# Where the copies, the sums of squares and the end of a rope stand in an attention layer on one core

## The chip, the cores and the metric

The kernel runs on one core of a Trainium2 chip. The metric is the device time of one execution in microseconds (us); less is better. The core has TensorE (PE in the profile, with its weight loads as PEld), VectorE (DVE), ScalarE (ACT), GpSimd (POOL) and SyncE (SP, used here only to issue DMAs). Each engine works through its own queue in order, and DMAs are issued as entries of such a queue.

## What is computed

An encoder trunk of two layers over 16 learned meta tokens and 512 tokens of width 2048 (T = 528): layer 0 is grouped-query softmax attention with 16 query heads, 8 key and value heads of width 128, normalised q and k and rotary positions; layer 1 is gated linear attention. The change is in layer 0 only, in how q and k are made:

```python
def _rotate(x, ang):
    cos, sin = jnp.cos(ang), jnp.sin(ang)          # per token
    x1, x2 = jnp.split(x, 2, axis=-1)
    return jnp.concatenate([x1 * cos - x2 * sin, x2 * cos + x1 * sin], axis=-1)
...
    q, k, v, gate = jnp.split(h @ w_in, [...], axis=-1)
    q = apply_axial_rope(rmsnorm(q, q_norm), ang_row, ang_col)
    k = apply_axial_rope(rmsnorm(k, k_norm), ang_row, ang_col)
    p = softmax(q @ k.T * ATTN_HEAD_DIM ** -0.5)
    return ((p @ v) * silu(gate)) @ w_out
```

`apply_axial_rope` rotates the first 64 of the 128 dimensions by the token's row and the last 64 by its column, so the partner of a dimension is the one 32 further or 32 back. `rmsnorm` divides by the root of the mean square over the 128 dimensions of a head.

## The kernel before

Every factor of a product is kept as a pair of tiles, high and low part (`uh`, `ul`; `split` writes the high part on ACT and the low part on DVE), and a product takes three matmuls. Activations lie transposed, 128 dimensions on the partitions and the 528 tokens along the row, in two halves of 264 (`HALVES`). `project` makes one block of 128 columns of `h @ w_in`: for each half a bank of PSUM (the chip has eight; `ps_p` is a ring of three of them, tag "pp"), 16 x 3 matmuls (L152 to L154), and then `evac`. Weights come in units of 8 k-blocks through `weights` (load L147 on SP's queue, split L129 on ACT and L130 on DVE), high and low parts in rings of three.

Attention goes over eight groups g, each with one key head and two query heads. While the softmax and the products of group g run (`attention`), `qkv(g + 1)` projects k, the first q and the second q of the next group, and then its v. Each of the three goes through `take` and `rope`: `evac` copies the block to `qw` and its squares to `sq` (L286, L287, on ACT); four DMAs (L294) copy `qw` with its blocks of 32 partitions swapped to `qs`; `sq` is split into `sh`, `sl`; POOL multiplies `qw` by the cosine (L299) and `qs` by the sine (L300). Two functions come later: `sums`, once per half, where PE adds the squares over the partitions (L304, L305, with a matrix of ones) and DVE reads the bank into `f` (L307); and `late`, which takes the inverse root on ACT (L133, L134), adds the two rotated parts (L311) and multiplies by the root (L312) on DVE, and splits the result into the tiles that attention reads (`kh`, `kl`, `qh`, `ql`). There are 24 ropes: three of the first group, whose blocks were projected at the kernel's start (`first_group`), and three in each `qkv`.

Attention of a group has 9 blocks of queries: the score product (L613 to L615, in the one pair of banks of `ps_s`, "s"), the maximum (L618), the exponential (L621), the scaling (L623, L624), the transposes (L631, L633, in a ring of two banks, `ps_t`, "t", which v's transposes use too), their split (L635, L636), and the product with v (L651 to L654) in `ps_o`, "o", which is a single bank. The sums of squares use that bank as well. Two gates per group are loaded from DRAM (L587), multiplied by the row's norm (L591), go through a SiLU (L137 to L139 on ACT, L601 on POOL), multiply the group's output (L595) and are stored (L596, on POOL's queue).

What is emitted when is set by `Clock`: `clk.step` moves a clock by the modelled time of each projection matmul, and `clk.after(dt, fn)` puts a function into the program once the clock has moved on by dt. The numbers in `rope`'s calls and the first value that `lead` yields (how long attention of a group waits for its start) are such times. The clock counts projection matmuls only, so a unit of it is longer than a microsecond wherever attention lies between. Behind that a scheduler sets the final order on each engine, and `tc.high_priority` lets an instruction go ahead of others.

Of the kernel before, what the change touches and what calls it, by code (L numbers as in the profile page):

```python
# [10 lines left out]
F32 = mybir.dt.float32  # L11
# [8 lines left out]
P = 128  # L20
# [7 lines left out]
HALVES = ((0, HALF), (HALF, T))  # L28
# [54 lines left out]
def hybrid_encoder(  # L83
# [5 lines left out]
    nc = tc.nc  # L89
    V, A, G, PE = nc.vector, nc.scalar, nc.gpsimd, nc.tensor  # L90
    clk = Clock()

    def pool(stack, name, bufs=1, **kw):
        return stack.enter_context(tc.tile_pool(name=name, bufs=bufs, reuse_waits="tile", **kw))
# [5 lines left out]
    ps_p = pool(ctx, "ps_p", 3, space=PSUM)  # L100
# [18 lines left out]
    def col(i):  # L119
        return cols[:, i:i + 1]  # L120
# [7 lines left out]
    def split(hi, lo, src):  # L128
        A.copy(hi, src)  # L129
        V.tensor_tensor(lo, src, hi.bitcast(F32), op=ALU.subtract)  # L130

    def rsqrt_inplace(t):
        A.activation(t, t, AF.Ln)  # L133
        A.activation(t, t, AF.Exp, scale=-0.5)  # L134
# [21 lines left out]
    def project(src, c0, parts, evac, last_k=None, ws=None):  # L156

        ws = ws or [weights(src[:, k0:k0 + 8, c0:c0 + P]) for k0 in (0, 8)]
        for a, b in parts:
            ps = ps_p.tile([P, 512], F32, tag="pp", name="pp")[:, :b - a]  # L160
            for k in range(KT):
                wh, wl = ws[k // 8]
                three(ps, wh[:, k % 8], wl[:, k % 8], k, a, b, k == 0, k == KT - 1)
                clk.step(3 * (b - a + 7) / 2400)
                if last_k and (a, b) == parts[-1]:
                    last_k(k)
            evac(ps, a, b)
# [111 lines left out]
    def take(wcol):  # L279

        qws.append(qws.pop(0))
        qw = qws[-1]
        sq = wk.tile([P, T], F32, tag="sq", name="sq")

        def evac(ps, a, b):
            A.activation(qw[:, a:b], ps, AF.Copy, scale=wcol)  # L286
            A.activation(sq[:, a:b], ps, AF.Square)  # L287
        return qw, sq, evac

    def rope(qw, sq, outs, steps):  # L290
        qs = wk.tile([P, T], F32, tag="qs", name="qs")
        for b in range(4):
            s = b ^ 1
            nc.scalar.dma_start(out=qs[b * 32:b * 32 + 32, :], in_=qw[s * 32:s * 32 + 32, :])  # L294
        sh = wk.tile([P, T], F32R, tag="sh", name="sh", bufs=1)
        sl = wk.tile([P, T], F32R, tag="sl", name="sl", bufs=1)
        split(sh, sl, sq)
        f = sq
        G.tensor_tensor(qw, qw, cos, op=ALU.mult)  # L299
        G.tensor_tensor(qs, qs, sin, op=ALU.mult)  # L300

        def sums(a, b):
            ps = ps_o.tile([P, 512], F32, tag="o", name="ssq")[:, :b - a]
            PE.matmul(ps, ones_r, sh[:, a:b], start=True, stop=False)  # L304
            PE.matmul(ps, ones_r, sl[:, a:b], start=False, stop=True)  # L305
            with tc.high_priority(AHEAD):
                V.scalar_tensor_tensor(f[:, a:b], ps, 1.0 / P, erow[:, a:b], op0=ALU.mult, op1=ALU.add)  # L307

        def late():
            rsqrt_inplace(f)  # L310
            V.tensor_tensor(qw, qw, qs, op=ALU.add)  # L311
            V.tensor_tensor(qw, qw, f, op=ALU.mult)  # L312
            for hi, lo, a, b in outs:
                split(hi, lo, qw[:, a:b])
        for step, part in zip(steps, HALVES):
            clk.after(step, lambda part=part: sums(*part))
        clk.after(8.3, late)

    def qk_tiles(p, n):
        kh, kl = [p.tile([P, T], F32R, name=f"k{w}{n}") for w in "hl"]  # L320

        qh, ql = [p.tile([P, 2 * T], F32R, name=f"q{w}{n}") for w in "hl"]
        outs = ([(kh, kl, 0, T)], [(qh[:, :T], ql[:, :T], 0, T)],
                [(qh[:, Q1:], ql[:, Q1:], 0, SEQ), (qh[:, T:Q1], ql[:, T:Q1], SEQ, T)])
        return (qh, ql, kh, kl), outs
    Q1 = T + META

    qws = [c0.tile([P, T], F32, name=f"qw{i}") for i in range(3)]
# [6 lines left out]
    ps_t = pool(st, "ps_t", 2, space=PSUM)  # L335
# [43 lines left out]
    accs, banks = [], []  # L379
    for i, (si, off) in enumerate(((0, 0), (1, 0), (1, P))):  # L380
        for j, (a, b) in enumerate(HALVES):
            n = 2 * i + j
            if n < 3:
                ps = ps_p.tile([P, 512], F32, tag="pp", name="pp")
            else:
                ps = ps_g.tile([P, 512], F32, name=f"g{n}")
            ps = ps[:, :b - a]
# [27 lines left out]
    ssq = sp.tile([P, 5, 4], F32, name="ssq")  # L415
# [103 lines left out]
    qks = [qk_tiles(pk, i) for i in range(2)]  # L519
# [3 lines left out]
    ps_t = pool(ps0, "ps_t0", 2, space=PSUM)  # L523
    ps_o = pool(ps0, "ps_o", space=PSUM)
# [15 lines left out]
    def values(g):  # L540
        vh = wa.tile([P, 4, P], F32R, tag="vh", name="vh")
        vl = wa.tile([P, 4, P], F32R, tag="vl", name="vl")
        vm = vm_bufs[g % 2]
        if g:
            project(w_in0, 3072 + g * P, HALVES, lambda ps, a, b: A.copy(vt[:, a:b], ps))

        def late():
            ps = ps_t.tile([P, 512], F32, tag="t", name="vps")
            for t in range(4):
                PE.transpose(ps[:, t * P:(t + 1) * P], vt[:, t * P:(t + 1) * P], ident)  # L550
            for t in range(4):
                pst = ps[:, t * P:(t + 1) * P]
                A.activation(vh[:, t, :], pst, AF.Copy, scale=rcol[:, t:t + 1])
                V.scalar_tensor_tensor(vl[:, t, :], pst, rcol[:, t:t + 1], vh[:, t, :].bitcast(F32),
                                       op0=ALU.mult, op1=ALU.subtract)
            pm = ps_t.tile([P, 512], F32, tag="t", name="vpm")[:META, :P]
            PE.transpose(pm, vt[:, SEQ:T], ident)
            rm = rcol[:META, 4:5]
            A.activation(vm[0:META], pm, AF.Copy, scale=rm)
            A.activation(vm[64:64 + META], pm, AF.Copy, scale=rm)  # L560
            V.scalar_tensor_tensor(vm[32:32 + META], pm, rm, vm[0:META].bitcast(F32),
                                   op0=ALU.mult, op1=ALU.subtract)
        clk.after(1.2 if g else 2.0, late)
        return vh, vl, vm

    def qkv(g):
        qk, outs = qks[g % 2]
        vv = values(g) if g == 1 else None
        for i, c in enumerate((2048 + g * P, 2 * g * P, (2 * g + 1) * P)):
            qw, sq, evac = take(col(KN if i == 0 else QN))  # L570
            project(w_in0, c, HALVES, evac)
            rope(qw, sq, outs[i], (4.4, 6.6))
        return qk, vv or values(g)

    def first_group():
        for i in range(3):
            sq = wk.tile([P, T], F32, tag="sq", name="sq")
            A.activation(sq, qws[i], AF.Square)
            A.activation(qws[i], qws[i], AF.Copy, scale=col(QN if i else KN))
            rope(qws[i], sq, qks[0][1][i], (2.6, 3.9))  # L580
            yield 4.2 if i < 2 else 9.0

    def stored_gates(hs, held):
# [104 lines left out]
    def o_tiles():  # L688
        return [wa.tile([P, T], F32, tag="o", name="o_sb", bufs=4) for _ in range(2)]
# [3 lines left out]
    for g in range(KV):  # L693
        o_sb = o_tiles()
        att = attention(qk, vv, o_sb, SLOTS[g])
        lead = first_group() if g == 0 else iter([8.5] if g == 1 else [])
        att = clk.drive(chain(lead, att))
        gates = [] if g == 0 else [2 * g - 2, 2 * g - 1]
        stored = clk.drive(stored_gates([h for h in gates if h < 13], held))
        if g + 1 < KV:  # L700
            nxt = qkv(g + 1)
        for h in gates:
            if h < 13:
                continue
            gs = gate(h)
            og = held[h % 2]
            V.tensor_tensor(og, og, gs, op=ALU.mult)
            nc.gpsimd.dma_start(out=og_d[h], in_=og)
        if g + 1 < KV:
            clk.finish(att, stored)  # L710
            qk, vv = nxt
            held = o_sb
# [28 lines left out]
    for m in range(2):  # L741
        for j, (a, b) in enumerate(HALVES):
            ps = (ps_t.tile([P, 512], F32, tag="t", name="po") if m and j else
                  ps_p.tile([P, 512], F32, tag="pp", name="pp"))[:, :b - a]
# [50 lines left out]
    ps_t = pool(tr, "ps_t1", space=PSUM)  # L795
# [24 lines left out]
    for i in range(2):  # L820
        for a, b in HALVES:
            ps = ps_g.tile([P, 512], F32, name=f"g{i}{a}")[:, :b - a]
# [109 lines left out]
    for a, b in HALVES:  # L932
        ps = ps_t.tile([P, 512], F32, tag="t", name="lrf")[:64, :b - a]
        PE.matmul(ps, fold, lt[:, a:b], start=True, stop=True)
        for d in range(2):
            pd, t = ps[d * 32:d * 32 + 16], lrs[d]
# [59 lines left out]
    ps_o = pool(ps1, "ps_o1", 2, space=PSUM)  # L996
# [335 lines left out]
    banks = [ps_p.tile([P, 512], F32, tag="pp", name="pp") for _ in range(3)]  # L1332
# [35 lines left out]
    for n, own in ((1, (s_, o_, o_, m_)), (2, (p_, p_, p_, s_)), (3, (s_, o_, o_, m_))):  # L1368
        banks = [p.tile([P, 512], F32, tag=tag, name="f") for p, tag in own]
# [45 lines left out]
```

## Time and profile before

| | |
|---|---|
| median of 3 runs | 1810.56 us (1808.33 to 1815.36) |
| the profiled execution | 1812.31 us, span 1810.6 us |
| mean granted clock of TensorE | 0.994 |
| share of the span | PE 97%, PEld 92%, DVE 62%, ACT 52%, POOL 12% |

The span goes from the first to the last instruction. In the rows that follow, a row of waits gives who waited for whom, the total in us, how often, and the longest; a row of the timeline gives the start, the duration, engine, line, operation, and in brackets how long its engine had been idle and what ended that; a row of a stretch gives its start and end, its length, the busy time of each engine with the number of instructions, the clock that TensorE was granted (1.00 is full speed), the share of the DMA engines and GB/s. SPq, ACTq and POOLq are the issuing side of those engines.

### The profile page before, as it was taken

What the parts mean: (1) busy time and instruction counts of PE and PEld (TensorE: products, weight loads), DVE (VectorE), ACT (ScalarE), POOL (GpSimd) and SP (SyncE); (2) the same over time, 40 slices, a digit from 0 to 9 for tenths busy, and PEclk for the clock granted to TensorE, in tenths of its full rate; (3) what the DMA queues carried; (4) which work ended last, traced back from release to release, by engine and by line L of the source; (5) the groups of instructions that cost most, each with busy time, mean ns of one, the idle gap of its engine ahead of it and who ended that gap; (6) DMA issues with size and microseconds to landing.
All of it is one profiled execution on the core that took longest, in us unless ns stands there. A gap on an engine that the chain in (4) does not pass through costs nothing.

```text
span 1810.6 us, 31594 instructions
## 1 busy us (share of the span) xinstructions
PE 1763.6 (97%) x12591; PEld 1660.6 (92%) x12591; DVE 1124.3 (62%) x1904; ACT 946.4 (52%) x1909; POOL 208.6 (12%) x270
## 2 busy tenths in 40 slices
PE   8999899999999999999999999999999999999998
PEld 8999899999999999999999999988898988888886
DVE  5877677666666666742229787668585865764224
ACT  5533465555555545542338544468675765853221
POOL 3000212111201111121111101110000100000000
PEclk9999999999999999999999999999999999999999
DMA  8444432233223323253236344343242332354323
GB/s 257 130 128 119 130 99 85 74 92 99 74 82 89 88 68 117 67 163 92 85 93 201 118 141 118 106 123 100 78 120 75 107 100 77 96 157 174 93 94 128
DMA packets 266788, 200.95 MB, mean 111 GB/s; under 512 B 9772, under 2 KB 239856, under 8 KB 266112
## 3 DMA queue, kind: packets, MB, share of 16 engines
q1 hardware_dynamic: 251888, 159.54, 30.6%
q0 software_dynamic: 10144, 32.90, 5.1%
q10 hardware_dynamic: 4608, 6.49, 1.3%
q8 instruction: 99, 1.62, 0.4%
q14 instruction: 49, 0.40, 0.1%
HBM read 164.39 MB, written 28.01 MB: 106 GB/s over the span
## 4 chain that ended last, share of the span: by engine, by line
PE 53%; DVE 3%; ACT 2%; DMA 1%; issue 1%; POOL 0%; ACTq 0%; DVEq 0%; POOLq 0%; SPq 0%
PE pp L152 10%; PE pp L154 10%; PE pp L153 9%; PE f L1327 2%; PE f L1325 2%; PE f L1326 2%; PE pp L229 2%; PE pp L230 2%; PE pp L231 2%; PE o L1145 1%; PE o L1146 1%; PE o L1144 1%; PE pp L1327 1%; PE pp L1325 1%; PE pp L1326 1%
## 5 line engine op out<-in xcount | busy, mean ns | idle before, releaser
L152 PE MATMUL pp<-uh,whi 128*128 128x264 f32 (+1 forms) x2320 | 714.3, 308 | 0.7 <-POOL whi L361 0.4
L153 PE MATMUL pp<-ul,whi 128*128 128x264 f32 (+1 forms) x2320 | 704.8, 304 | 0.6 <-DVE ul L423 0.6
L154 PE MATMUL pp<-uh,wlo 128*128 128x264 f32 (+1 forms) x2320 | 704.6, 304 | 0.4 <-POOL wlo L362 0.3
L130 DVE TENSOR_TENSOR wlo<-wraw,whi 128x1024 fp32r<-128x1024 f32 (+1 forms) x239 | 291.3, 1220 | 298.3 <-ACT whi L129 297.1
L152 PEld LDWEIGHTS pp<-uh,whi 128*128 128x128 f32 x2320 | 439.4, 189 | 17.2 <-POOL whi L361 0.7
L154 PEld LDWEIGHTS pp<-uh,wlo 128*128 128x128 f32 x2320 | 439.1, 189 | 17.4 <-POOL wlo L362 0.6
L153 PEld LDWEIGHTS pp<-ul,whi 128*128 128x128 f32 x2320 | 439.7, 190 | 14.6 <-DVE ul L423 1.0
L129 ACT CAST whi<-wraw 128x1024 fp32r<-128x1024 f32 (+1 forms) x239 | 248.7, 1042 | 289.6 <-PE pp L153 99.5
L129 ACT CAST whi<-x 128x1024 fp32r<-128x1024 f32 x48 | 50.1, 1046 | 69.6 <-PE pp L230 53.8
L621 ACT ACTIVATE pn<-s,mx 128x528 f32<-128x528 f32 (+1 forms) x72 | 50.2, 697 | 51.2 <-DVE mx L618 50.5
L1327 PE MATMUL f<-whi,ul 128*128 128x512 f32 x192 | 75.6, 394 | 0.0
L1325 PE MATMUL f<-whi,uh 128*128 128x512 f32 x192 | 75.6, 394 | 0.0
L1326 PE MATMUL f<-wlo,uh 128*128 128x512 f32 x192 | 75.4, 393 | 0.0
L231 PE MATMUL pp<-uh,wlo 128*128 128x264 f32 x264 | 75.3, 285 | 0.0
L229 PE MATMUL pp<-uh,whi 128*128 128x264 f32 x264 | 75.1, 284 | 0.0
L230 PE MATMUL pp<-ul,whi 128*128 128x264 f32 x264 | 74.8, 283 | 0.0
L130 DVE TENSOR_TENSOR wlo<-x,whi 128x1024 fp32r<-128x1024 f32 x48 | 58.6, 1223 | 23.6 <-ACT whi L129 23.5
L299 POOL TENSOR_TENSOR qw<-qw,cos 128x528 f32<-128x528 f32 x24 | 32.4, 1349 | 342.2 <-DMA qs<-qw 278.3
L618 DVE TENSOR_REDUCE mx<-s 128x1 f32<-128x528 f32 (+1 forms) x72 | 50.7, 704 | 12.6 <-PE s L615 11.0
L229 PE MATMUL pp<-th,whi 128*128 128x264 f32 x192 | 56.2, 293 | 1.3 <-ACT th L129 1.3
L230 PE MATMUL pp<-tl,whi 128*128 128x264 f32 x192 | 54.6, 285 | 0.0
L231 PE MATMUL pp<-th,wlo 128*128 128x264 f32 x192 | 54.4, 284 | 0.0
(402 smaller groups left out, 3692.2 us busy)
## 6 DMA issues: line engine op xcount, KB each, us to landing
wraw<-in_attn_w_in_dram SPq DMA_DIRECT2D x82, 512.0 KB, 4.2
wraw<-in_gla_w_in_dram SPq DMA_DIRECT2D x81, 512.0 KB, 3.9
wraw<-in_attn_w_out_dram SPq DMA_DIRECT2D x32, 512.0 KB, 3.8
wraw<-in_gla_w_out_dram SPq DMA_DIRECT2D x32, 512.0 KB, 3.9
x<-in_gla_w_in_dram SPq DMA_DIRECT2D x15, 512.0 KB, 4.3
qs<-qw ACTq DMA_DIRECT2D x96, 66.0 KB, 3.9
x<-in_attn_w_in_dram SPq DMA_DIRECT2D x12, 512.0 KB, 4.3
x<-h_d SPq DMA_DIRECT2D x32, 132.0 KB, 2.9
```

The lines of the kernel that those rows point to most:

```text
L129: A.copy(hi, src)
L130: V.tensor_tensor(lo, src, hi.bitcast(F32), op=ALU.subtract)
L152: PE.matmul(ps, wh, uh[:, k, a:b], start=first, stop=False)
L153: PE.matmul(ps, wh, ul[:, k, a:b], start=False, stop=False)
L154: PE.matmul(ps, wl, uh[:, k, a:b], start=False, stop=last)
L229: PE.matmul(ps, w[0][:, k], bh[:, k], start=k == 0, stop=False)
L230: PE.matmul(ps, w[0][:, k], bl[:, k], start=False, stop=False)
L231: PE.matmul(ps, w[1][:, k], bh[:, k], start=False, stop=k == KH - 1)
L618: V.reduce_max(mx, s, axis=AX.XY, negate=True)
L1325: PE.matmul(ps, uh[:, k, ts], wh[:, kk], start=(k == 0), stop=False)
L1326: PE.matmul(ps, uh[:, k, ts], wl[:, kk], start=False, stop=False)
L1327: PE.matmul(ps, ul[:, k, ts], wh[:, kk], start=False, stop=(k == KT - 1))
```

## The change

The four copies of a rope are issued on POOL's queue; the two sums of a rope in `qkv` take a bank each from the ring of the projections, at 3.2 and 8.8 units of the clock behind the projection's end in place of 4.4 and 6.6; `late` comes at 9.6 in place of 8.3. In `first_group` the times stay (2.6, 3.9 and 8.3), and the two sums take `ps_o` and the transposes' ring. Attention of group 1 starts at 4.0 in place of 8.5.

```diff
-    def rope(qw, sq, outs, steps):
+    def rope(qw, sq, outs, steps, banks):
...
-            nc.scalar.dma_start(out=qs[b * 32:b * 32 + 32, :], in_=qw[s * 32:s * 32 + 32, :])
+            nc.gpsimd.dma_start(out=qs[b * 32:b * 32 + 32, :], in_=qw[s * 32:s * 32 + 32, :])
...
-        def sums(a, b):
-            ps = ps_o.tile([P, 512], F32, tag="o", name="ssq")[:, :b - a]
+        def sums(bank, a, b):
+            ps = bank[0].tile([P, 512], F32, tag=bank[1], name="ssq")[:, :b - a]
...
-        for step, part in zip(steps, HALVES):
-            clk.after(step, lambda part=part: sums(*part))
-        clk.after(8.3, late)
+        for step, bank, part in zip(steps, banks, HALVES):
+            clk.after(step, lambda bank=bank, part=part: sums(bank, *part))
+        clk.after(steps[2], late)
...
-            rope(qw, sq, outs[i], (4.4, 6.6))
+            rope(qw, sq, outs[i], (3.2, 8.8, 9.6), ((ps_p, "pp"), (ps_p, "pp")))
...
-            rope(qws[i], sq, qks[0][1][i], (2.6, 3.9))
+            rope(qws[i], sq, qks[0][1][i], (2.6, 3.9, 8.3), ((ps_o, "o"), (ps_t, "t")))
...
-        lead = first_group() if g == 0 else iter([8.5] if g == 1 else [])
+        lead = first_group() if g == 0 else iter([4.0] if g == 1 else [])
```

Since the times steer a scheduler, the order on the engines moves in more places than the diff names. On POOL, in `qkv` of a middle group (the one whose second query's L300 lies at 493.5 us in the timeline of before; `qw1` and `qw2` are the first and the second query's blocks), before:

```order
L299 TENSOR_TENSOR qw1_95<-qw1_95,cos_2402 128x528
L300 TENSOR_TENSOR qs_5593<-qs_5593,sin_2403 128x528
L299 TENSOR_TENSOR qw2_96<-qw2_96,cos_2402 128x528
L300 TENSOR_TENSOR qs_5810<-qs_5810,sin_2403 128x528
L596 DMA og_d_70<-o_sb_5115 128x528
L601 TENSOR_TENSOR gs_7104<-gs_7104,gr_6902 128x528
L596 DMA og_d_70<-o_sb_5116 128x528
```

and now:

```order
L294 DMA qs_5593<-qw1_95 32x528 x4
L299 TENSOR_TENSOR qw1_95<-qw1_95,cos_2402 128x528
L300 TENSOR_TENSOR qs_5593<-qs_5593,sin_2403 128x528
L294 DMA qs_5810<-qw2_96 32x528 x4
L596 DMA og_d_70<-o_sb_5115 128x528
L601 TENSOR_TENSOR gs_7104<-gs_7104,gr_6902 128x528
L299 TENSOR_TENSOR qw2_96<-qw2_96,cos_2402 128x528
L300 TENSOR_TENSOR qs_5810<-qs_5810,sin_2403 128x528
L596 DMA og_d_70<-o_sb_5116 128x528
```

The copies stand ahead of the two products of their rope, and one store and one gate product have moved between the second query's copies and its L299.

On DVE, at the end of the same second query's rope (the first row is the reading of its first sum), before:

```order
L307 SCALAR_TENSOR_TENSOR sq_5604<-ssq_5901,erow_92 128x264
L636 TENSOR_TENSOR pl_5553<-pT_5884,ph_5552 128x4x128
L311 TENSOR_TENSOR qw2_96<-qw2_96,qs_5810 128x528
L307 SCALAR_TENSOR_TENSOR sq_5604<-ssq_5928,erow_92 128x264
L312 TENSOR_TENSOR qw2_96<-qw2_96,sq_5604 128x528
L591 TENSOR_TENSOR gr_7779<-gr_7779,rrow_91 128x528
L130 TENSOR_TENSOR wlo_6003<-wraw_6001,whi_6002 128x1024
```

and now:

```order
L307 SCALAR_TENSOR_TENSOR sq_5604<-ssq_5881,erow_92 128x264
L636 TENSOR_TENSOR pl_5553<-pT_5888,ph_5552 128x4x128
L311 TENSOR_TENSOR qw2_96<-qw2_96,qs_5810 128x528
L591 TENSOR_TENSOR gr_7779<-gr_7779,rrow_91 128x528
L595 TENSOR_TENSOR o_sb_5116<-o_sb_5116,gs_6409 128x528
L130 TENSOR_TENSOR wlo_6003<-wraw_6001,whi_6002 128x1024
L307 SCALAR_TENSOR_TENSOR sq_5604<-ssq_5961,erow_92 128x264
L130 TENSOR_TENSOR wlo_6212<-wraw_6210,whi_6211 128x1024
L312 TENSOR_TENSOR qw2_96<-qw2_96,sq_5604 128x528
L618 TENSOR_REDUCE mx_6018<-s_6011 128x1
L554 SCALAR_TENSOR_TENSOR vl_5822<-vps_6038,rcol_93,vh_5821 128x128
```

The reading of the second sum and the product with the root have moved back, behind a gate's two products and the splits of two weight units.

On DVE, in the k rope that is issued while the first group's attention runs (`qw0` is the key's block, `pl` the low part of a transposed block of probabilities), before:

```order
L307 SCALAR_TENSOR_TENSOR sq_2616<-ssq_2902,erow_92 128x264
L622 RECIPROCAL sm_2861<-sm_2861 128x1
L311 TENSOR_TENSOR qw0_94<-qw0_94,qs_2799 128x528
L623 TENSOR_SCALAR pn2_2408<-pn2_2408,sm_2861 128x512
L624 TENSOR_SCALAR pn2_2408<-pn2_2408,sm_2861 128x3x16
L636 TENSOR_TENSOR pl_2828<-pT_2879,ph_2827 128x4x128
```

and now:

```order
L623 TENSOR_SCALAR pn2_2408<-pn2_2408,sm_2861 128x512
L307 SCALAR_TENSOR_TENSOR sq_2616<-ssq_2893,erow_92 128x264
L624 TENSOR_SCALAR pn2_2408<-pn2_2408,sm_2861 128x3x16
L636 TENSOR_TENSOR pl_2828<-pT_2879,ph_2827 128x4x128
L311 TENSOR_TENSOR qw0_94<-qw0_94,qs_2799 128x528
L618 TENSOR_REDUCE mx_2916<-s_2909 128x1
```

The scaling of a block and the split of the transposed one have moved ahead of L311.

## The prediction

> **What bounds the kernel now.** I read the page's first part, then busy time by stage, then what TensorE waits for in the one stage that the change touches, and last the timeline around the longest of those waits.
>
> ```profile
> span 1810.6 us, 31594 instructions
> PE 1763.6 (97%) x12591; PEld 1660.6 (92%) x12591; DVE 1124.3 (62%) x1904; ACT 946.4 (52%) x1909; POOL 208.6 (12%) x270
> ```
>
> TensorE (PE) is the bound: whatever doesn't shorten its idle time or its clock is worth nothing. By stage (columns: stretch, length, busy time of each engine, granted clock, DMA):
>
> ```profile
> 60.00:205.00 145.00, 145.00 (x1194) 145.00 (x1193) 116.04 (x139) 59.19 (x72) 8.43 (x17) 1.00 0.41 120
> 205.00:775.00 570.00, 542.16 (x4363) 533.48 (x4362) 379.30 (x749) 313.94 (x710) 93.74 (x80) 0.99 0.31 91
> 775.00:950.00 175.00, 175.00 (x1440) 174.87 (x1440) 47.09 (x49) 57.93 (x103) 30.65 (x33) 1.00 0.36 103
> ```
>
> The stages before and behind are full, and they are left as they are. The attention stage, 205 to 775 us, is the one with ropes in it: PE is idle there for 570 - 542.2 = 27.8 us. That is the purse. What ended the idle time (total, times, longest):
>
> ```profile
> PE o L651 <- DVE sq L307: 9.8, 5, 3.2
> PE pT L631 <- DVE pl L636: 4.4, 3, 3.0
> PE ssq L304 <- DVE sq L307: 3.7, 6, 1.7
> PE s L613 <- ACT pn L621: 2.9, 2, 2.6
> PE ssq L305 <- DVE sl L130: 2.3, 1, 2.3
> PE pTm L633 <- DVE vl L554: 2.0, 2, 1.1
> PE ssq L304 <- ACT sh L129: 1.2, 1, 1.2
> ...
> ```
>
> Rows 1 and 3 are one thing: the single bank of ps_o holds the sums of squares and the attention output in turn, and VectorE (DVE) has to empty it at L307 before PE may write it again. Why DVE is late there shows at the longest wait:
>
> ```profile
> 493.52 1.33 POOL L300 TENSOR_TENSOR qs<-qs,sin 128x528 f32<-128x528 f32 x1
> 494.78 0.58 POOL L596 DMA_DIRECT2D og_d<-o_sb  x1
> 494.89 2.37 DVE L311 TENSOR_TENSOR qw<-qw,qs 128x528 f32<-128x528 f32 x1 [2.58 <-POOL qs L300]
> 495.38 1.31 POOL L601 TENSOR_TENSOR gs<-gs,gr 128x528 f32<-128x528 f32 x1
> 497.29 0.43 DVE L307 SCALAR_TENSOR_TENSOR sq<-ssq,erow 128x264 f32<-128x264 f32 x1
> 497.87 0.57 PE L651 MATMUL o<-ph,vh 128*128 128x272 f32 x1 [3.23 <-DVE sq L307]
> 500.50 0.69 DVE L130 TENSOR_TENSOR ql<-qw,qh 128x512 fp32r<-128x512 f32 x1
> ```
>
> DVE stands 2.58 us at L311, then takes 2.37 us for it beside a POOL instruction, and only then reads the second half of the sums, for which PE has waited 3.23 us. The waits also cost clock:
>
> ```profile
> 224.20:227.60 3.40, 3.40 (x17) 3.40 (x17) 3.38 (x5) 3.24 (x5) 0.17 (x1) 0.51 0.03 5
> 306.20:309.50 3.30, 3.30 (x18) 3.30 (x17) 2.36 (x7) 0.96 (x3) 0.00 (x0) 0.50 0.71 224
> 497.30:500.70 3.40, 2.83 (x12) 2.86 (x13) 1.95 (x4) 1.90 (x3) 0.00 (x0) 0.50 0.26 80
> 708.90:712.30 3.40, 3.30 (x14) 3.33 (x15) 1.32 (x2) 1.90 (x3) 0.00 (x0) 0.50 0.00 0
> ```
>
> ```profile
> 223.24 0.39 PE L305 MATMUL ssq<-sl,ones_r 128*128 128x264 f32 x1 [2.31 <-DVE sl L130]
> 305.71 0.39 PE L613 MATMUL s<-kh,qh 128*128 128x264 f32 x1 [2.64 <-ACT pn L621]
> 709.00 0.57 PE L651 MATMUL o<-ph,vh 128*128 128x272 f32 x1 [2.07 <-DVE sq L307]
> ```
>
> Each of these four stretches of 3.4 us has a clock of 0.50 and lies at the end of a wait: of 2.31, 2.64, 3.23 (the timeline before) and 2.07 us. Half of the busy time in them, (3.40 + 3.30 + 2.83 + 3.30) / 2 = 6.4 us, is work that full speed would not have needed.
>
> **The change part by part.** *Banks.* After the first group, a rope's two sums go to the ring of three that the projections use; L651 is alone on ps_o, and its two rows, 9.8 and 3.7 us, lose their cause: 13.5 us. The ring has room: between two halves of a projection lies one sum, so a bank comes round after three allocations. A half is 48 matmuls, 48 x 145.0 / 1194 = 5.8 us by the first stage row, and what frees a bank is a reading of 0.43 us (L307) or the two copies of a finished half. Bounds 0 to 13.5 gained; I take 13.5, because by the order the second L307 also stands three rows further back on DVE, behind a weight split, but no longer in front of L651.
>
> *First group.* Its second sum goes to the ring of two of the transposes; the 1.7 us of row 3 (counted already) goes. The 2.3 + 1.2 us at L305 and L304 come from a late split, with four copies being issued on ScalarE's (ACT's) queue ahead of it. Bounds 0 to 3.5; I take 2.5, as the split's own DVE part stays slow beside POOL.
>
> *Copies on POOL's queue.* 96 issues leave ACT and join POOL:
>
> ```profile
> L294 ACTq DMA_DIRECT2D qs<-qw x96: 514/602/1714, 205.8 to 700.6; - x96
> DMA to landing us min/median/max: 1.9/3.9/6.3
> ```
>
> ```profile
> L596 POOL DMA_DIRECT2D og_d<-o_sb x13: 543/581/583, 287.0 to 742.7; - x13
> DMA to landing us min/median/max: 2.4/2.4/3.6
> ```
>
> For ACT that is 96 x 0.60 = 58 us of issue time less, for POOL 96 x 0.58 = 56 us more on 94 of 570 us busy. ACT is not the bound, so I book nothing for it beyond the sh split just named. How long a copy from SBUF to SBUF takes from POOL no row shows: between 2.4 (POOL's own, larger, to DRAM) and 3.9 us (the same copy from ACT), with 1.9 and 6.3 as outer ends. I take 3.9, the same bytes, so the rope's chain keeps its length. That chain, in the k rope of a middle group:
>
> ```profile
> 448.99 2.44 ACTq L294 DMA_DIRECT2D qs<-qw  x4
> 455.14 1.32 POOL L299 TENSOR_TENSOR qw<-qw,cos 128x528 f32<-128x528 f32 x1 [19.08 <-DMA qs<-qw]
> 457.78 0.71 DVE L311 TENSOR_TENSOR qw<-qw,qs 128x528 f32<-128x528 f32 x1 [3.19 <-POOL qs L300]
> 459.25 0.69 ACT L621 ACTIVATE pn<-s,mx 32x528 f32<-32x528 f32 x1 [5.22 <-DVE mx L618]
> 461.78 0.28 PE L613 MATMUL s<-kh,qh 128*128 128x264 f32 x1
> ```
>
> 8.8 us from the first issue to L311, of which DVE stands 3.19. Behind that stop waits the maximum of a softmax, then L621, which frees the score bank for L613: from 459.94 to 461.78 there are 1.8 us to spare. Moved past the copies on POOL's queue are L596 and L601: in the second query's rope they now lie between the copies and L299, 0.58 + 1.33 = 1.9 us that fit into the landing of 3.9. What waits for L601 is the next gate's load on SyncE:
>
> ```profile
> SPq L587 <- POOL gs L601: 62.6, 11, 9.8
> ```
>
> It comes earlier there, not later, so the weights behind it on that queue don't suffer. And L601 no longer runs beside L311: 2.37 - 0.71 = 1.7 us of DVE time at that place is returned.
>
> *Ends later.* `late` at 9.6 for 8.3 puts other DVE work ahead of L311. In the k rope issued during the first group the order has the split of the transposed block, L636, now in front of L311; the 3.0 us of pT waiting for pl there (the longest of row 2; the rest of the row lies in the last group and stays) and the 2.9 us of row 4 behind the same kind of stop should mostly go. Bounds 0 to 5.9; I take 4.0. The second query's rope ends nearer to its use, but from the second L307 to the last split is 501.19 - 497.29 = 3.9 us, and the first product of the second head stands some 45 projection matmuls behind the second sum, 45 x 0.121 = 5.4 us: covered, and without that cover a wait of 1 to 4 us once per group.
>
> *Lead 4.0 for 8.5 in one group.* The same work in another interleaving; the same 5.4 against 3.9 us covers it, and bare it would cost one wait like that of 2.6 us in row 4. I book 0, bounds -2.6 to +2.6.
>
> *Clock.* With the waits go the half-speed stretches: 4.5 of 6.4 us, since a new wait may bring one of them back. [...]
>
> *What is late next.* At the boundary of two groups the order puts a root (L134) ahead of the copy of v on ACT and a maximum (L618) ahead of the last vl split on DVE. The nearest row is pTm waiting for vl, 2.0 us in two of seven boundaries. Bounds 0 and 7 x 2.6; I take 7 x 1.0, of which 2.0 are paid already: +5.0.
>
> Sum: -13.5 - 2.5 - 4.0 - 4.5 + 5.0 = -19.5 us. The profiled execution took 1812.3 us (span 1810.6 and 1.7 around it), so 1792.8; its time lies 1.75 us over the median of the runs shown (1810.56), which would put the median at 1791. I say 1792.
>
> **The rivals.** *POOL late (slower).* Every us by which L300 ends later than now is a us more in which DVE stands at L311. By the k rope 1.8 us of that are free, and then each of 24 ropes pays: time = 1792 + 24 x (D - 1.8). It eats the whole gain at D = 1.8 + 19.5 / 24 = 2.6 us and is slower by over 0.5% from about D = 3.0; at the copy's slowest landing, 6.3 (D = 2.4), it gives 1806; with as much again for the POOL work that now stands between, D = 4.3, 1852. For it: four issues one after the other on a queue that also computes. Against: the landing of 2.4 to 3.6 us of POOL's own stores while DVE was busy for two thirds of the stage. [...] Chance 0.10.
>
> *A wait in place of the old one.* The bank is free, but DVE's stops at L311 stay (48.8 us over 20 times in all, see the row), and PE, arriving earlier, meets them at the next product:
>
> ```profile
> DVE qw L311 <- POOL qs L300: 48.8, 20, 3.7
> ```
>
> If each of seven boundaries pays the mean of L651's waits, 9.8 / 5 = 2.0, in place of 1.0, and the clock stays as it is: 1792 + 7.0 + 4.5 = 1803.5; with the first group and pT waits back too (6.5), 1810. For it: in this stage five kinds of waits already hang on DVE. Against: by the order L307, L636 and the weight splits now pass ahead of L311 or of what follows it. Chance 0.18.
>
> *More than forecast.* All 27.8 us and the clock go: 1812.3 - 27.8 - 6.4 = 1778. Chance 0.03; every group would have to run without any wait.
>
> **How the numbers follow.** Forecast 0.69 (its own range 1781 to 1802), a wait in place of the old one 0.18 (1803 to 1812), POOL late 0.10, more 0.03. Half a per cent, 9 us, is what a measurement of this kernel can tell from no change (the runs before spread over 7 us). Faster: 0.66 of the forecast, 0.03 and 0.01 of the second case, 0.70. Same: 0.03 + 0.17 + 0.02 = 0.22. Slower: 0.08. The range from 1780 to 1808 leaves out the upper half of the second case, most of POOL late and the largest gain.
>
> **What would show it.** Right: no row of PE at L651 or L304 waiting for L307; PE idle under 15 us in the stage; at most two half-speed stretches there; qs landing from POOL near 4 us or less; L311's stops no longer than 3.7 us; ACT without L294; new rows for vps, vl or pTm at the boundaries. Wrong: L311 waiting over 5 us each time, or a projection matmul waiting for L307 in the shared ring, or PE idle still over 22 us under other names.

## The result, and the profile after

| | median of all runs | range |
|---|---|---|
| before | 1812.11 us (4 runs) | 1808.33 to 1815.36 |
| after | 1796.45 us (4 runs) | 1794.34 to 1797.7 |

The ratio is 0.9913, 95% interval 0.9890 to 0.9936: faster by 15.7 us. The profiled execution of the changed kernel took 1796.57 us, against 1812.31 us before. The number forecast (1792, range 1780 to 1808) holds; the experiments show that several of the terms behind it do not. That their errors cancel is luck.

From the page the busy times, and the row of the attention stage (the same columns as before):

```profile
PE 1759.3 (98%) x12591; PEld 1655.3 (92%) x12591; DVE 1120.7 (62%) x1904; ACT 946.6 (53%) x1909; POOL 256.6 (14%) x366
```

```profile
205.00:775.00 570.00, 553.80 (x4497) 545.15 (x4496) 389.04 (x765) 322.00 (x723) 147.78 (x183) 0.99 0.33 98
```

POOL is 48 us busier, which is 96 issues of 0.50 us. PE's idle time in the stage is 570 - 553.8 = 16.2 us, where it was 27.8. What ended it (`vt` is ACT's copy of v, `vps` the bank in which it is transposed, `vl` the low part of v, `vm` its rows for the meta tokens, `pn` the exponentials, `pT` and `pTm` the transposed probabilities, `sh` and `sl` the two parts of the squares):

```profile
PE ssq L305 <- DVE sl L130: 5.5, 6, 2.9
PE s L613 <- ACT pn L621: 4.3, 6, 1.7
PE ssq L304 <- DVE vm L561: 2.6, 2, 2.1
PE pT L631 <- DVE pl L636: 1.4, 2, 1.2
PE ssq L304 <- DVE sq L307: 1.2, 1, 1.2
PE pTm L633 <- DVE vl L554: 0.6, 2, 0.3
PE vps L550 <- ACT vt L545: 0.5, 1, 0.5
```

The row of L651 waiting for L307 (9.8 us) is gone, and the split of the squares (L305 waiting for L130) is now the first. Of the half-speed stretches two are left in the stage, where there were five (the four shown ahead and one from 743.1 us); both lie in the first group, behind waits of 2.10 and 2.88 us:

```profile
216.30:219.70 3.40, 3.40 (x18) 3.40 (x17) 2.69 (x6) 1.61 (x5) 1.39 (x3) 0.51 0.85 264
229.90:233.30 3.40, 2.71 (x12) 2.71 (x13) 3.34 (x5) 2.39 (x5) 1.90 (x2) 0.52 0.54 155
```

```profile
215.97 0.39 PE L304 MATMUL ssq<-sh,ones_r 128*128 128x264 f32 x1 [2.10 <-DVE vm L561]
230.59 0.59 PE L305 MATMUL ssq<-sl,ones_r 128*128 128x264 f32 x1 [2.88 <-DVE sl L130]
```

Idle time in the stage's 570 us fell by 11.6 us. Half of PE's busy time in half-speed stretches fell from (3.40 + 3.30 + 2.83 + 3.30 + 3.40) / 2 = 8.1 to (3.40 + 2.71) / 2 = 3.1 us, so by 5.0. Together that is an estimate of 16.6 us, for 15.7 measured.

Now the second query's rope of the same middle group, which the prediction showed at 493 us. The rows come from the timeline of the changed kernel, all engines, in order of time:

```profile
482.70 2.01 POOL L294 DMA_DIRECT2D qs<-qw  x4 [10.70 <-ACT sq L287]
...
487.19 1.33 POOL L601 TENSOR_TENSOR gs<-gs,gr 128x528 f32<-128x528 f32 x1 [1.04 <-ACT gs L139]
489.75 1.31 POOL L300 TENSOR_TENSOR qs<-qs,sin 128x528 f32<-128x528 f32 x1
489.98 0.29 PE L651 MATMUL o<-ph,vh 128*128 128x272 f32 x1
491.10 0.71 DVE L311 TENSOR_TENSOR qw<-qw,qs 128x528 f32<-128x528 f32 x1 [2.48 <-POOL qs L300]
491.73 0.70 DVE L591 TENSOR_TENSOR gr<-gr,rrow 128x528 f32<-128x528 f32 x1
492.70 0.28 PE L304 MATMUL ssq<-sh,ones_r 128*128 128x264 f32 x1
494.44 0.43 DVE L307 SCALAR_TENSOR_TENSOR sq<-ssq,erow 128x264 f32<-128x264 f32 x1
```

DVE still stops at L311 for 2.48 us, nearly as long as before (2.58). But PE has begun the output product (L651, 489.98) ahead of that stop, and the second sum (L304, 492.70) comes only behind the product; its late reading at 494.44 holds up nobody. L601 runs ahead of L300, in the time in which the copies land, and L311 takes 0.71 us where it took 2.37 beside L601.

### The profile page after: what moved, and what is told of

It reads as the page before. It is cut to its first block, busy times and chain, and to the rows that moved or that the text cites. A ratio compares the mean times of both kernels' runs of the same rounds, so it can differ in the third digit from the quotient of the medians.

```text
span 1794.8 us, 31607 instructions
## 1 busy us (share of the span) xinstructions
PE 1759.3 (98%) x12591; PEld 1655.3 (92%) x12591; DVE 1120.7 (62%) x1904; ACT 946.6 (53%) x1909; POOL 256.6 (14%) x366
## 5 line engine op out<-in xcount | busy, mean ns | idle before, releaser
L130 DVE TENSOR_TENSOR wlo<-wraw,whi 128x1024 fp32r<-128x1024 f32 (+1 forms) x239 | 292.8, 1226 | 289.6 <-ACT whi L129 286.7
L294 POOL DMA_DIRECT2D qs<-qw x96 | 48.5, 510 | 246.9 <-ACT sq L287 212.3
L130 DVE TENSOR_TENSOR wlo<-x,whi 128x1024 fp32r<-128x1024 f32 x48 | 58.6, 1222 | 22.1 <-ACT whi L129 22.1
L311 DVE TENSOR_TENSOR qw<-qw,qs 128x528 f32<-128x528 f32 x24 | 20.0, 835 | 69.1 <-POOL qs L300 69.1
L636 DVE TENSOR_TENSOR pl<-pT,ph 128x512 fp32r<-128x512 f32 (+1 forms) x80 | 47.4, 592 | 16.5 <-ACT ph L635 15.6
```

## The experiments

Ratios are to the kernel before, on the same chip, with 95% intervals. The first four ran on one chip, the next four on a second, the last four on a third.

| kernel | edit | ratio |
|---|---|---|
| banks_only | before + the ring for the later ropes' sums | 0.9954 (0.9939 to 0.9969) |
| copies_only | before + copies on POOL | 1.0072 (1.0060 to 1.0084) |
| times_only | before + 3.2, 8.8, 9.6 and 4.0 | 0.9919 (0.9906 to 0.9933) |
| after_one_bank | after, later ropes' sums in ps_o | 0.9901 (0.9886 to 0.9915) |
| second_later | before + second sum at 8.8, end at 9.6 | 0.9934 (0.9910 to 0.9958) |
| lead_only | before + start of group 1 at 4.0 | 1.0024 (1.0006 to 1.0043) |
| after_act_copies | after, copies on ACT | 0.9952 (0.9935 to 0.9968) |
| after_copies_twice | after, each copy issued twice | 1.0059 (1.0035 to 1.0082) |
| second_later_pool | second_later + copies on POOL | 0.9932 (0.9911 to 0.9952) |
| after_first_pp | after, first group's sums in the ring too | 0.9903 (0.9883 to 0.9924) |
| after_sum36 | after, first sum at 3.8 | 0.9932 (0.9910 to 0.9954) |
| after_lead85 | after, start of group 1 at 8.5 | 0.9937 (0.9917 to 0.9957) |

My theory at first, A in the expectations, was the prediction's: the bank that the sums share with the output product is the cause, so the ring brings the gain. B was the issue time that leaves ACT, C the new times.

**banks_only.** The kernel before with the ring alone; times, copies and lead as before.

```diff
-            rope(qw, sq, outs[i], (4.4, 6.6))
+            rope(qw, sq, outs[i], (4.4, 6.6, 8.3), ((ps_p, "pp"), (ps_p, "pp")))
```

> Theory A (the single bank of ps_o, shared by the sums and the attention output, is what PE waits for): the ring alone, with the copies still on ACT and the old times, takes away all rows of PE at L651 or L304 waiting for L307 behind the first group, about 12 us, and two half-speed stretches, 3 us: 1796 to 1801. Theory B (the copies' issue time on ACT makes everything late) and theory C (the times 8.8 and 9.6, which put other work ahead of L311) expect under 4 us from the ring alone: 1808 to 1813.

Measured 1807.14 us, before 1815.48: 0.46% faster, about half of the change's 0.87%, and between the theories' ranges (A up to 1801, B and C from 1808). The first rows of what PE waits for:

```profile
PE pTm L633 <- DVE vl L554: 5.3, 3, 2.7
PE pT L631 <- DVE pl L636: 4.8, 4, 3.2
```

L651's row is gone, as the ring must have it. PE then meets DVE at the next products: vl and pl together cost 10.1 us, where they cost 6.4 before. That is the second rival of the prediction, in part.

**copies_only.** The kernel before with `nc.gpsimd.dma_start` at L294.

```diff
-            nc.scalar.dma_start(out=qs[b * 32:b * 32 + 32, :], in_=qw[s * 32:s * 32 + 32, :])
+            nc.gpsimd.dma_start(out=qs[b * 32:b * 32 + 32, :], in_=qw[s * 32:s * 32 + 32, :])
```

> Only the issuing queue of the copies changes. Theory B: a gain of 10 us or more, 1797 to 1802, since 58 us of issue time leave ACT. Theory A: within 4 us of before, 1808 to 1816, L651 still waiting for L307 for some 10 us, since the bank is still shared and DVE still stops at L311.

Measured 1828.53 us: slower by 0.72%, 13 us, which neither theory had in its range. The first wait of PE, and then rows from the timeline of the second query's rope:

```profile
PE o L651 <- DVE sq L307: 17.2, 5, 3.9
```

```profile
490.74 0.49 ACT L286 ACTIVATE qw<-pp,cols 128x264 f32<-128x264 f32 x1
...
499.67 0.71 DVE L311 TENSOR_TENSOR qw<-qw,qs 128x528 f32<-128x528 f32 x1 [2.59 <-POOL qs L300]
500.29 0.70 DVE L591 TENSOR_TENSOR gr<-gr,rrow 128x528 f32<-128x528 f32 x1
501.03 0.43 DVE L307 SCALAR_TENSOR_TENSOR sq<-ssq,erow 128x264 f32<-128x264 f32 x1
501.61 0.42 PE L651 MATMUL o<-ph,vh 128*128 128x272 f32 x1 [3.20 <-DVE sq L307]
```

The rope is no longer than before: L311 starts 8.93 us behind the copy of the finished half (L286), before it was 9.07, so the landing is not at fault. What moved is PE: it starts the second sum (496.81 us) 6.07 us behind L286, where before it was 7.32. It comes earlier to the same stop of DVE, with both sums still ahead of the output product, and the gate's product L591 now stands between L311 and the second L307. In this group L651 waits as long as before (3.20 against 3.23 us, though L311 takes 0.71 us in place of 2.37); in the four others it waits 3.1 to 3.9 us, where it waited 1.4 to 2.1. Why the ropes lie later against PE was not traced to its start.

**times_only.** The kernel before with the new times alone; both sums of every rope stay in ps_o, the copies on ACT.

```diff
-            rope(qw, sq, outs[i], (4.4, 6.6))
+            rope(qw, sq, outs[i], (3.2, 8.8, 9.6), ((ps_o, "o"), (ps_o, "o")))
...
-        lead = first_group() if g == 0 else iter([8.5] if g == 1 else [])
+        lead = first_group() if g == 0 else iter([4.0] if g == 1 else [])
```

> Only the times change (3.2, 8.8, 9.6, and 4.0 for the start of group 1), with the sums still in ps_o and the copies on ACT. Theory C: a gain of 8 us or more, since L307 and the splits pass ahead of L311's stop. Theory A: 1806 to 1816, the sums further apart but still in the bank of the attention output, so waits at L651 or at L304 stay near 10 us in sum.

Measured 1801.57 us, 0.81% faster: nearly the whole gain without the ring. L651 waits for L307 0.4 us in all, though the bank is shared as before. That is what theory C expected, and not A.

**after_one_bank.** The changed kernel with the later ropes' sums in ps_o again.

```diff
-            rope(qw, sq, outs[i], (3.2, 8.8, 9.6), ((ps_p, "pp"), (ps_p, "pp")))
+            rope(qw, sq, outs[i], (3.2, 8.8, 9.6), ((ps_o, "o"), (ps_o, "o")))
```

> The changed kernel with the sums of the later ropes back in ps_o (copies on POOL, new times, the first group as changed). Theory A: the gain is lost for the most part, 1805 to 1813, with rows at L651 or L304 waiting for L307 again. Theories B and C: it stays at 1795 to 1800.

Measured 1796.92 us, ratio 0.9901, and the changed kernel has 0.9913: the same. With the new times and the copies on POOL the ring is worth nothing that can be measured. Theory A fell.

What the times do in its place stands in the order of PE. In the kernel before, and in banks_only and copies_only, the second query's rope reads: first sum, 21 projection matmuls, second sum, 9 more, then the output product. With the second sum at 8.8 the output product lies between the two sums. It then needs the bank behind the first reading only, which DVE does ahead of L311. This is theory D: what counts is whether the product stands behind the second sum. A bank of its own takes L651's wait away too (banks_only), but it brought half of the gain.

**second_later.** The kernel before with the second sum and the end moved, and nothing else.

```diff
-            rope(qw, sq, outs[i], (4.4, 6.6))
+            rope(qw, sq, outs[i], (4.4, 8.8, 9.6))
```

> The kernel before with one difference: in the later ropes the second sum comes at 8.8 and the end at 9.6 (first sum 4.4, bank ps_o, copies on ACT, group 1 from 8.5, all as before). By the order PE now has the output product between the two sums of the second query's rope, no longer behind both. Theory D (which of the two sums stands ahead of the output product decides: the second one is read behind L311's stop, the first ahead of it): no row of L651 waiting for L307 above 1 us in sum, and most of the gain of the times, ratio 0.991 to 0.996. Theory E (the earlier first sum or the earlier start of group 1 does it): ratio 0.997 or more.

Measured 1800.01 us, before 1812.45: 0.66% faster, three quarters of the gain from two numbers. First two rows of the kernel before, where the second sum (493.14) stands ahead of the product that the prediction showed at 497.87 us:

```profile
490.95 0.43 DVE L307 SCALAR_TENSOR_TENSOR sq<-ssq,erow 128x264 f32<-128x264 f32 x1
493.14 0.28 PE L304 MATMUL ssq<-sh,ones_r 128*128 128x264 f32 x1
```

and now second_later, PE and DVE:

```profile
488.50 0.28 PE L304 MATMUL ssq<-sh,ones_r 128*128 128x264 f32 x1
489.36 0.43 DVE L307 SCALAR_TENSOR_TENSOR sq<-ssq,erow 128x264 f32<-128x264 f32 x1
492.41 0.29 PE L651 MATMUL o<-ph,vh 128*128 128x272 f32 x1
493.63 2.42 DVE L311 TENSOR_TENSOR qw<-qw,qs 128x528 f32<-128x528 f32 x1 [2.91 <-POOL qs L300]
495.14 0.28 PE L304 MATMUL ssq<-sh,ones_r 128*128 128x264 f32 x1
499.03 0.43 DVE L307 SCALAR_TENSOR_TENSOR sq<-ssq,erow 128x264 f32<-128x264 f32 x1
```

L311 stops for longer than before (2.91 us) and takes 2.42 us; PE passes by without a wait, in the same single bank; L651's waits for L307 are 0.4 us in all. Ratio and waits lie where theory D had them. The two numbers were not run apart, so what the later end adds to the later sum stays open.

**lead_only.** The kernel before with attention of group 1 at 4.0.

```diff
-        lead = first_group() if g == 0 else iter([8.5] if g == 1 else [])
+        lead = first_group() if g == 0 else iter([4.0] if g == 1 else [])
```

> The kernel before with only the start of group 1's attention at 4.0 in place of 8.5. Theory D: L651 waits for L307 as before, ratio 0.998 to 1.002. Theory E, for the start: ratio 0.997 or less.

Measured 1816.36 us, 0.24% slower. L651's waits grow from 9.8 to 13.8 us; in the old order the earlier start only adds to them. The ratio, 1.0024, lies just over theory D's range, which ended at 1.002.

**after_act_copies.** The changed kernel with the copies on ACT's queue.

```diff
-            nc.gpsimd.dma_start(out=qs[b * 32:b * 32 + 32, :], in_=qw[s * 32:s * 32 + 32, :])
+            nc.scalar.dma_start(out=qs[b * 32:b * 32 + 32, :], in_=qw[s * 32:s * 32 + 32, :])
```

> The changed kernel with the copies back on ACT's queue (new times, sums in the shared ring). Theory D: the ring is worth nothing beside the times, so this is like the times alone, ratio 0.991 to 0.994, with PE waiting for L545 and L636 again (ACT's late work at the boundaries); POOL's queue is worth 2 to 5 us here. Theory G (ring and times together already give all of it, the copies nothing): ratio 0.9895 to 0.991 and none of those waits.

Measured 1803.75 us, 0.9952: it lacks about 0.4% of the changed kernel's gain, 7 us (the intervals just touch), and lies in neither theory's range (up to 0.994 for D, up to 0.991 for G). PE waits for v's copy and for pl again:

```profile
PE vps L550 <- ACT vt L545: 7.1, 5, 2.5
PE pT L631 <- DVE pl L636: 6.1, 5, 4.0
```

The timeline at the longest wait for vt shows a chain that goes through all engines:

```profile
497.29 1.33 POOL L300 TENSOR_TENSOR qs<-qs,sin 128x528 f32<-128x528 f32 x1
499.16 1.40 POOL L601 TENSOR_TENSOR gs<-gs,gr 128x528 f32<-128x528 f32 x1
500.58 0.34 SPq L587 DMA_DIRECT2D gr<-g_d  x1
503.25 0.71 DVE L591 TENSOR_TENSOR gr<-gr,rrow 128x528 f32<-128x528 f32 x1 [2.13 <-DMA gr<-g_d]
504.00 0.43 DVE L307 SCALAR_TENSOR_TENSOR sq<-ssq,erow 128x264 f32<-128x264 f32 x1
504.46 0.64 ACT L133 ACTIVATE sq<-sq 128x528 f32<-128x528 f32 x1 [1.99 <-DVE sq L307]
...
507.03 0.35 ACT L545 COPY vt<-pp 128x264 f32<-128x264 f32 x1
507.43 0.44 PE L550 MATMUL vps<-ident,vt 128*128 128x128 f32 x2 [2.45 <-ACT vt L545]
```

With the copies on ACT the gate's product L601 stands behind L300. The next gate's load waits for L601, DVE waits 2.13 us for that load, the second L307 stands behind it, the inverse root (L133, then L134) behind that, and v's copy behind L134. In the changed kernel L601 comes 2.6 us ahead of L300, L591 doesn't wait, and the whole chain is gone. So part of what POOL's queue brings here is the place of L601. This was read from the two traces; L601 alone was not moved.

One comparison stays unexplained. times_only has its copies on ACT too, but the sums in ps_o, and it has 0.9919, against 0.9952 here; the intervals do not meet, though the chips differ. So with the copies on ACT the new banks seem to cost 0.3%, and PE waits 7.1 us for vt where it waits 5.1 in times_only. That the ring is worth nothing was measured with the copies on POOL alone.

**after_copies_twice.** The changed kernel with the same four copies issued twice, on the same queue; the second four write the same data and wait for the first (at L294 POOL waits 61.9 us for copies in all, in 38 waits).

```diff
-        for b in range(4):
+        for b in (0, 1, 2, 3, 0, 1, 2, 3):
```

> The changed kernel with each rope's four copies issued twice, the same data again: four issues of 0.50 us more on POOL ahead of L299, so L300 ends some 2 us later or more. By the prediction's price for a late POOL, 24 x (D - 1.8) with D from 2.0 to 2.5: 5 to 17 us slower than the changed kernel, ratio to before 0.994 to 1.001, L311's stops 115 us or more in sum. If the room behind L311 is larger now that no sum of this rope is waited for by the output product: ratio 0.990 to 0.993 with the same longer stops.

Measured 1822.67 us, ratio 1.0059, some 26 us over the changed kernel and above what was expected (up to 1.001). From the end of the copy of a block's second half (L287) to the end of L300 the 21 later ropes take 8.49 us on the mean in the kernel before, 8.54 in the changed one, and 11.51 here. The prediction's price for a chain longer by 11.51 - 8.54 = 3.0 us was 24 x (3.0 - 1.8) = 29 us. The sum comes near, but not in the prediction's way, by which DVE would stand that much longer at L311: L311's stops are 61.7 us in all, against 69.1 in the changed kernel, and 115 or more were expected. PE's largest waits are for ACT:

```profile
PE ssq L304 <- ACT sh L129: 11.0, 6, 4.0
PE vps L550 <- ACT vt L545: 9.3, 6, 3.0
```

On ACT the inverse root L133 waits 57.5 us for L307, against 31.4 in the changed kernel, and the next block's copies and split stand behind it. The POOL time of the second issues, an estimated 96 x 0.50 = 48 us by the changed kernel's issues, is part of this cost and cannot be taken out of it.

**second_later_pool.** second_later with the copies on POOL.

```diff
-            rope(qw, sq, outs[i], (4.4, 6.6))
+            rope(qw, sq, outs[i], (4.4, 8.8, 9.6))
...
-            nc.scalar.dma_start(out=qs[b * 32:b * 32 + 32, :], in_=qw[s * 32:s * 32 + 32, :])
+            nc.gpsimd.dma_start(out=qs[b * 32:b * 32 + 32, :], in_=qw[s * 32:s * 32 + 32, :])
```

> The kernel before with only two lines changed: a later rope's second sum at 8.8 and its end at 9.6 (first sum stays at 4.4, both sums in ps_o, attention of group 1 at 8.5), and the copies on POOL's queue. Theory D (what counts is that the output product no longer stands behind the second sum, and POOL's queue then takes the copies' issue time from ACT at the boundaries): like the changed kernel, ratio 0.990 to 0.993, no more than 2 us of waits of PE at L651 for L307, vps waiting for vt below 2 us in place of 5.1. Rival (the ring, the earlier first sum or the earlier start of group 1 carry a part): 0.994 or more. Rival (POOL's queue costs what it cost alone, +0.7%): 1.000.

Measured 1801.38 us, before 1815.31: 0.9932, the same as second_later (0.9934). The copies on POOL, which cost 0.72% in the old order, cost nothing in the new one, but they bring nothing either without the earlier start and the earlier first sum. The ratio lies between theory D's range (up to 0.993) and its rival's (from 0.994). The remaining quarter of the gain, as far as the runs can tell it (the intervals overlap), lies in the three together. L651's waits for L307 are gone, as D had it, but PE waits for vt 6.1 us, six times at 1.2 us or less, where D expected under 2. DVE's waits for a gate have shrunk from 9.9 to 1.4 us, so they can't account for vt's 6.1.

**after_first_pp.** The changed kernel with the first group's sums in the ring too.

```diff
-            rope(qws[i], sq, qks[0][1][i], (2.6, 3.9, 8.3), ((ps_o, "o"), (ps_t, "t")))
+            rope(qws[i], sq, qks[0][1][i], (2.6, 3.9, 8.3), ((ps_p, "pp"), (ps_p, "pp")))
```

> The changed kernel with the two sums of each rope of the first group in the projections' ring as well, in place of ps_o and the transposes' ring. If the first group's 6.7 us of waits come from the bank that the second sum takes (a transposes' bank, emptied behind vm at L561), the rows of L304 waiting for vm (2.6 us) and for L307 (1.2 us) go and about 3 us are gained, 0.2%. If they come from the split of the squares and from what stands on DVE in any case, another row of the same size takes their place, and the time stays within 0.1% of the changed kernel.

Measured 1795.74 us, 0.9903: not to be told from the changed kernel. The longest of the first group's waits there:

```profile
216.96 0.39 PE L152 MATMUL pp<-uh,whi 128*128 128x264 f32 x1 [2.27 <-DVE sq L307]
```

The wait of 2.10 us for vm became one of 2.27 us of a projection matmul for L307 in the ring. The first group's waits are 4.9 us in all, against 6.7, which is too little to show in the time. In either ring PE meets DVE.

**after_sum36.** The changed kernel with the first sum at 3.8.

```diff
-            rope(qw, sq, outs[i], (3.2, 8.8, 9.6), ((ps_p, "pp"), (ps_p, "pp")))
+            rope(qw, sq, outs[i], (3.8, 8.8, 9.6), ((ps_p, "pp"), (ps_p, "pp")))
```

> The changed kernel with a later rope's first sum at 3.8 in place of 3.2. Five waits of 0.5 us of the second query's first sum for the low part of the squares (L305 for L130) should go: 1.5 to 2.5 us, 0.1%. If DVE's split moves back with it, nothing changes.

Measured 1800.78 us, 0.9932; a gain was expected, and it is 5 us slower than after_first_pp on the same chip.

```profile
PE s L613 <- ACT pn L621: 6.7, 7, 1.7
PE vps L550 <- ACT vt L545: 4.2, 4, 1.3
```

The five small waits for sl went (5.5 to 2.9 us), and four for vt (4.2 us against 0.5) and more for pn (6.7 against 4.3) came.

**after_lead85.** The changed kernel with attention of group 1 at 8.5.

```diff
-        lead = first_group() if g == 0 else iter([4.0] if g == 1 else [])
+        lead = first_group() if g == 0 else iter([8.5] if g == 1 else [])
```

> The changed kernel with attention of group 1 started at 8.5 again, as before. The prediction booked nothing for the 4.0, with ends of 2.6 us on either side. Alone on the kernel before it cost 4 us (0.24%). If that holds here, this kernel is 0.2% faster than the changed one; if the start matters only through the old order, the same within 0.1%; if the changed order needs the earlier start, slower, with one more wait of 2 to 3 us of the score product.

Measured 1802.1 us (1801.27 to 1803.27), 0.9937: 6 us slower than after_first_pp on the same chip (1794.61 to 1798.74), which equals the changed kernel. The score product waits again at the place of row 4 of before (there 2.64 us at 305.71):

```profile
304.42 0.39 PE L613 MATMUL s<-kh,qh 128*128 128x264 f32 x1 [2.33 <-ACT pn L621]
```

In the stage there are four half-speed stretches of 3.4 us, where the changed kernel has two. The same number that cost 0.24% in the old order is worth about 0.3% in the new one. None of the twelve beats the changed kernel by more than the runs can tell; after_one_bank and after_first_pp equal it.

## Why the prediction was right, and where it was not

**Banks, -13.5.** The two rows did lose nearly all of their 13.5 us (1.2 are left, in the first group). The step that failed is the reason: "L651 is alone on ps_o, and its two rows, 9.8 and 3.7 us, lose their cause". The ring alone brings 8 us (banks_only), and nothing once the second sum stands behind the output product (after_one_bank). The prediction named the second L307 "no longer in front of L651" as a side effect of the bank; it is the place of the sum on PE that does this (second_later), and the prediction looked at DVE's order there and not at PE's. The new times were costed as "Ends later" only, at -4.0; alone they bring 14 us.

**First group, -2.5.** Failed. Its waits in the kernel before are 1.66 + 1.23 + 2.31 = 5.2 us; after they are 2.10 + 1.20 + 2.88 + 0.51 = 6.7. The 1.7 us of row 3 became 2.10 us for vm, since the transposes' ring is emptied by v's own work. The split of sl did not come sooner with ACT's issues gone. What was booked as its slow DVE part is 1.81 us in the kernel before, at 221.38 us beside POOL's L299 and L300; the split for which PE waits 2.88 us in the changed kernel has no POOL instruction beside it and takes 0.69 us, at 229.85 us.

**Copies, 0.** The landing taken (3.9 us) was right, and so was the chain's length:

```profile
L294 POOL DMA_DIRECT2D qs<-qw x96: 496/498/707, 205.8 to 690.0; - x96
DMA to landing us min/median/max: 1.8/4.0/6.4
```

Issue costs 0.50 us, estimated 0.58. The 1.7 us at L311 came back as stated, and L587 comes earlier; but the value was not nothing. The step that failed is "ACT is not the bound, so I book nothing": with the new times and the ring the copies are worth some 7 us (after_act_copies), in ps_o some 5 (times_only at 1801.57 against after_one_bank at 1796.92, which differ in one bank of the first group too, and whose intervals overlap), and in the old order they cost 13. The gate's load is one way to that value, the row of pT, below, another. The 96 issues on POOL have a median of 0.498 us and a longest of 0.707 us, with DVE busy for 389 of the stage's 570 us.

**Ends later, -4.0.** The step that failed is "`late` at 9.6 for 8.3 puts other DVE work ahead of L311", as the reason why two rows would go. The 3.0 us of pT did go (4.4 to 1.4), but by the copies. With the later end and the copies on ACT the row stays, in times_only:

```profile
PE pT L631 <- DVE pl L636: 5.6, 5, 3.1
```

In copies_only, with the old end, it is 1.4 us, as in the changed kernel: there DVE has L623, L624 and L636 ahead of L311 in the k rope that is issued during the first group, and in times_only behind it, as before. The row of s waiting for pn grew from 2.9 to 4.3 us, in six waits of at most 1.7. Its one long wait of 2.64 us is 4.03 in second_later, with the later end; in the changed kernel it is 1.72, and in after_lead85 2.33, so it was the earlier start that shortened it. What second_later gained shows at L651, whose waits for L307 fell from 9.8 to 0.4 us.

**Lead, 0.** Its bounds were 2.6 us either way. In the new order it is worth more, 4 to 6 us (0.9937 against 0.9913 and 0.9903), 0.6 us of row 4's wait and its half-speed stretch among them.

**Clock, -4.5.** Right in kind: of the four stretches shown 3.3 of 6.4 us went net, and 1.7 us with the fifth, so 5.0. The two stretches that are left lie behind waits of 2.10 and 2.88 us.

**What is late next, +5.0.** Wrong sign in the rows it named: vps waiting for vt and pTm waiting for vl cost 2.8 us before and 1.1 after. Where the copies stay on ACT the forecast waits are there, 7.1 us for vt alone. In the changed kernel new waits came elsewhere: five of 0.5 us at L305 for sl, and those for pn.

**The rivals.** POOL late did not happen (8.54 us from L287 to L300, against 8.49). Its price came near when the chain was made longer, 26 us for 29, but by luck: the stops at L311 that it counts did not grow. The wait in place of the old one happened in banks_only, and not in the whole change, where the times move the product as well. Of the marks named ahead, four failed: PE's idle time is 16.2 us and not under 15, one wait of L304 for L307 is left, vps and pTm show no new waits, and L311's stops are longer, up to 5.0 us:

```profile
DVE qw L311 <- POOL qs L300: 69.1, 23, 5.0
```

DVE stops 20 us more there, and PE's idle time fell all the same. In the rope shown, what stands behind the stop (the second sum's reading) holds up nobody; for the other ropes this was not followed.

## What to carry over

When one engine waits for a bank, look at the order on the waiting engine first: whether it must pass the late reading at all may be a matter of where the writing stands, and a new bank is then not needed. The parts of such a change do not add up: the same copies cost 0.7%, nothing, or bring 0.4% according to the times beside them, and the same start costs 0.2% or brings 0.3%. So price a moved instruction by what stands behind it in the new order of every queue, and undo it from the whole as well as doing it alone.

## What the hardware showed

In the attention stage of the kernel before and of the changed one PE runs in seven stretches of 3.3 to 3.4 us at a clock of 0.50 to 0.52. Six lie behind waits of 2.07 to 3.23 us, and the one from 743.1 us of the kernel before behind a wait of 1.16 us (L631 at 741.50). The length of the wait alone does not decide. In the kernel before PE waits

```profile
256.89 0.63 PE L631 MATMUL pT<-ident,pn 128*128 128x128 f32 x4 [3.04 <-DVE pl L636]
```

and keeps full speed (clock 1.00 from 255.0 to 262.4 us), where half speed goes with a wait of 2.07 us at 709.0 us (0.50 from 708.9 to 712.3 us). At the last group's L631 PE waits 1.17 us in the changed kernel and keeps full speed (1.00 from 727.0 to 740.0 us), and 1.16 us in after_lead85 and runs at half speed some 1.2 us later (0.50 from 733.0 to 735.0 us). What else decides was not tried.

In the kernel before a DVE sum of two 128x528 tiles (L311) takes 0.70 or 0.71 us wherever no POOL instruction runs beside it, 19 times of 24. At 494.89 us, where POOL's L601 starts 0.49 us behind it, it takes 2.37 us. But that is not so each time: 70 us earlier L601 starts 0.50 us behind L311 as well, and

```profile
424.20 0.71 DVE L311 TENSOR_TENSOR qw<-qw,qs 128x528 f32<-128x528 f32 x1 [2.44 <-POOL qs L300]
```

So beside L601 the sum took 1.7 us more in the one place and nothing more in the other; what decides between the two was not tried.
